# Gates' staging and the top keys' scratch in the solver's spent table

## Chip, core and metric

The kernel runs on one core of a Trainium2 chip. The metric is the device time of one launch in microseconds. TensorE (PE) does the matmuls, VectorE (DVE), ScalarE (ACT) and GpSimd (POOL) the rest; SyncE (SP) and POOL's queue issue transfers.

## The reference, cut to what matters

One decoder block on 512 tokens of width 1024. One projection of the normalised input, `w_in`, gives the columns of three parts: an RWKV-7 token mixer (8 heads of 64), a sparse attention whose keys an indexer chooses, and 2 x 1024 columns of sigmoid gates. Then come cross attention into 256 memory tokens and a mixture of experts.

```python
sa = einsum('bhij,bhj->bhi', state, -kk_t)                  # RWKV: one step per token
state = state * w_t + sa[..., None] * (kk_t * a_t) + v_t[..., None] * k_t
y_t = einsum('bhij,bhj->bhi', state, r_t)                   # then a norm per head, x g
score[t, s] = sum_h w_idx[t, h] * relu(q_idx[t, h] . k_idx[s])   # indexer, 4 heads of 64
keys(t) = the 128 largest scores among s <= t               # min(256, L/4) of L = 512
h = h + (ya @ w_pa * sigmoid(ga + ba) + yb @ w_pb * sigmoid(gb + bb)) @ w_out
```

## The kernel before

**The projections.** `w_in` is used in blocks of 128 columns: 1024 x 128 weights are loaded by SP into a ring of three raw slots in the region "rawring" (`E` in the code), split into a high half by ACT (L197 CAST) and a low half by DVE or, for odd gates, by POOL (L197 TENSOR_TENSOR) into the region "xparts" (`RX`), and multiplied by 24 matmuls of 128x512 (L230).

**The solver.** RWKV runs over 8 chunks of 64 tokens. For each chunk PE does L704 and L710 (right-hand side from the table `AA` and the state), DVE copies it out (L713), PE applies the inverse from the same table `AA` (L716), DVE and ACT each copy half of the answer (L719), and PE forms outputs and the next state (L727, L732), which DVE takes out (L742, L743). `AA` holds for four pairs of heads, all chunks and both heads a 64-column block; L716 of a chunk is the last reader of its blocks. After two chunks each, a group norm runs on DVE and ACT (L753 to L759); PE then transposes y in batches (L768, L157) and multiplies in g2 (L774).

**The indexer.** For query tiles 1, 2 and 3 PE computes scores against 256, 384 and 512 keys (L489), ACT takes the relu (L490), DVE weighs and adds the four heads (L493, L495), POOL masks (L497), and DVE finds the largest keys in 16 rounds of MAX (L501) and MATCH_REPLACE (L502); MAX writes eight values into a scratch tile `m8s`.

**The gates.** Sixteen blocks of columns: projections, tanh on ACT into one of two tiles `gst` (L589), and a transfer to DRAM (`gate_d`, L590) that POOL's queue issues. Between two gates the code lets the indexer go on by three steps (`pace`). Two later parts also use `gst`: the sparse attention's queries (`copy_out`, L777) and keys.

**The memory's norm.** `mem_norm` loads the 256 memory tokens and the vector `norm_mem` (L567) and normalises on DVE (L193).

**Reuse.** Then the regions "rawring" and "xparts" close, and the memory side's regions "early" and "memory" lie over the same bytes. The first load into them is w_uk (L797, on SP), then w_uv and the blocks of w_ck and w_cv; PE transposes the memory (L810) and uses w_uk in L517. A tile of the new regions waits for the last use of every old tile that its bytes overlap, and the regions are tiles as a whole.

**The order.** The instructions of each engine are put in order ahead of time by a scheduler that follows the data dependences and bank use; the program's text gives priorities only. So a changed buffer changes the order on every engine.

Of the kernel before, what the change touches and what calls it, by code (L numbers as in the profile page):

```python
# [8 lines left out]
AF = mybir.ActivationFunctionType  # L9
# [4 lines left out]
T, D, P = 512, 1024, 128  # L14
# [73 lines left out]
def build(tc, I, out):  # L88
    nc = tc.nc
    V, S, G, PE = nc.vector, nc.scalar, nc.gpsimd, nc.tensor  # L90
# [10 lines left out]
    gate_d = park.tile([2, 4, P, 2, T], F32, name="gate_d")  # L101
# [5 lines left out]
    def region(stack, name, n, dt, side=None):  # L107
        return Mem(stack.enter_context(tc.tile_pool(name=name, bufs=1, side=side)).tile([P, n], dt, name=name), n)
# [5 lines left out]
    def psum(tag="mm"):  # L114

        i = turn.get(tag, 0)
        turn[tag] = i + 1
        return PS[:, banks[tag][i % len(banks[tag])], :]
# [117 lines left out]
    E = region(front, "rawring", NX + NK - NR1, F32)  # L236
# [50 lines left out]
    def projT(nb):  # L287
        with tc.issue_after(roots[NT - 1][0]):
            w = ring1.load(I["w_in"][nb], G if nb % 2 else V)
        pt = psum()  # L290
        for k in range(KD):
            mm3(pt[:, :], lambda x: w[:, x, k * P:(k + 1) * P], lambda x: xn[:, k // 4, x, k % 4, :], k == 0, k == KD - 1)
        return pt
# [14 lines left out]
    omm = M.get(14)  # L308
# [8 lines left out]
    hb = M.get(16)  # L317
# [10 lines left out]
    AA = M.get(4, NCH, 2, 64)  # L328
# [121 lines left out]
    bias = {0: cb}  # L450
# [31 lines left out]
    def indexer(qt):  # L482
        nk = (qt + 1) * P
        isc = isc_[qt]
        for h in range(4):
            hr = slice((h % 2) * 64, (h % 2) * 64 + 64)
            rel = rels[h % 2]
            pt = psum("at")
            PE.matmul(pt[:, 0:nk], qiT[hr, h // 2, qt * P:(qt + 1) * P], kiT[hr, 0:nk], start=True, stop=True)  # L489
            S.activation(rel[:, 0:nk], pt[:, 0:nk], AF.Relu)  # L490
            wh = cw[:, qt, P + h:P + h + 1]
            if h == 0:
                V.tensor_scalar(isc[:, :], rel[:, 0:nk], wh, 0.0, op0=OP.mult, op1=OP.add)  # L493
            else:
                V.scalar_tensor_tensor(isc[:, :], rel[:, 0:nk], wh, isc[:, :], op0=OP.mult, op1=OP.add)  # L495
            yield
        G.affine_select(isc[:, qt * P:], isc[:, qt * P:], pattern=[[-1, P]], compare_op=OP.is_ge, fill=NEG, base=0,  # L497
                        channel_multiplier=1)
        m8 = m8s[qt - 1]
        for r in range(16):  # L500
            V.max(m8[:, r, :], isc[:, :])  # L501
            V.match_replace(isc[:, :], m8[:, r, :], isc[:, :], -2.0e38)  # L502
            if r % 2:
                yield
        V.tensor_scalar(isc[:, :], isc[:, :], -2.0e38, BIG, op0=OP.not_equal, op1=OP.mult)
        bias[qt] = isc
        yield
# [56 lines left out]
    def mem_norm():  # L564
        nm, raw = M.get(2, D), E.get(2, D)
        gmem = rels_[:, :]
        nc.sync.dma_start(gmem, I["norm_mem"].partition_broadcast(P))  # L567
        for i in range(2):
            nc.sync.dma_start(raw[:, i, :], I["mem"][i * P:(i + 1) * P, :])
        for i in range(2):  # L570
            norm_tile(nm[:, i, :], raw[:, i, :], gmem)
        raw.done()
        return nm

    def chained(*gens):
        for g in gens:
            yield from g

    def pace(gen, blocks, per):

        for b in blocks:
            b()
            for _ in range(per):
                next(gen, None)

    def gate(nb):
        pt = projT(22 + nb)
        g_ = gst[nb % 2]
        S.activation(g_.ap, pt[:, :], AF.Tanh, scale=0.5, bias=hb[:, nb:nb + 1])  # L589
        nc.gpsimd.dma_start(gate_d[nb // 8, nb % 8 // 2, :, nb % 2, :], g_.ap)  # L590

    def copy_out(nb, dst):
        pt = projT(nb)
        (S.copy if nb % 2 else V.tensor_copy)(dst, pt[:, :])
# [89 lines left out]
    gst = [E.get(T) for _ in range(2)]  # L684
    isc_ = {qt: M.get((qt + 1) * P) for qt in range(1, NT)}
    inverse()
    rels_ = E.get(2 * T)
    rels, m8s = [rels_[:, i * T:i * T + T] for i in range(2)], [E.get(16, 8) for _ in range(3)]
    g2 = M.get(4 * P)
    nc.sync.dma_start(g2[:, :], I["g2"])  # L690

# [6 lines left out]
    for c in range(NCH):  # L698
# [3 lines left out]
        for hp, q in heads:  # L702
            with behind(*first.values()):
                r = PE.matmul(px[own[1 - q], hp * 64:hp * 64 + 64], AA[own[q], hp, c, q, :],  # L704
                              ZV[own[q], c, hp * P + q * 64:hp * P + q * 64 + 64], start=hp == 0, stop=True,
                              skip_group_check=hp > 0)
# [17 lines left out]
        for hp, q in heads:  # L724
            os_ = slice(q * 256 + hp * 64, q * 256 + hp * 64 + 64)
            with behind(*first):
                r = PE.matmul(po[:, os_], ST[:, hp, c, q * 128:q * 128 + 128], ZV[:, c, hp * P + q * 64:hp * P + q * 64 + 64],  # L727
                              start=not first, stop=True, skip_group_check=bool(first))
# [35 lines left out]
    for hp in range(4):  # L764
        pt = psum("rw")
# [14 lines left out]
    latent(projT(17))  # L780
    for i in range(2):
        copy_out(14 + i, qiT[:, i, :])
    bg = chained(*[indexer(qt) for qt in range(1, NT)])
    pace(bg, [lambda i=i: gate(i) for i in range(16)], 3)
    for _ in bg:
        pass
    nm = mem_norm()
    for x in (hb, *gst, rels_, *m8s, omm):
        x.done()
    front.close()  # L790

# [80 lines left out]
    for x, (src, wsrc) in enumerate(((yaT, I["w_pa"]), (ybT, I["w_pb"]))):  # L872
        for k in range(4):
            split(act[:, x, 0, k, :], act[:, x, 1, k, :], src[:, k, :])
        for j in range(4):
# [5 lines left out]
            for n in range(2):  # L881
                nb = j * 2 + n
                pt = psum()
# [604 lines left out]
    with tc.manual_schedule(engines={PE.engine}):  # L1488
# [5 lines left out]
        for p in range(16):  # L1494
# [12 lines left out]
            if p == OVER * 2 + 1:  # L1507
                e = p * 2 + 2
# [80 lines left out]
```

## Time and profile before

| | us |
|---|---|
| median of 3 runs (lowest, highest) | 1271.01 (1266.04, 1273.87) |
| profiled execution: time | 1261.12 |
| profiled execution: span | 1259.3 |
| PE busy, share of the span | 1186.5, 94% |
| DVE busy, share | 647.8, 51% |
| ACT busy, share | 366.6, 29% |
| POOL busy, share | 111.1, 9% |

The span is cut in time by stages: the solver's chunks run from about 230 to 300 us, the gates with the rest of the indexer to 387, the memory side and the sparse attention after it, the experts from about 780 on. In the rows, times count from the span's start; "[1.78 <-DVE xparts L197]" behind an instruction says that its engine stood idle for 1.78 us and what ended that. PEclk is the share of full TensorE clock that was granted. L numbers are lines of the kernel before.

### The profile page before, as it was taken

What the parts mean: (1) busy time and instruction counts of PE and PEld (TensorE: products, weight loads), DVE (VectorE), ACT (ScalarE), POOL (GpSimd) and SP (SyncE); (2) the same over time, 40 slices, a digit from 0 to 9 for tenths busy, and PEclk for the clock granted to TensorE, in tenths of its full rate; (3) what the DMA queues carried; (4) which work ended last, traced back from release to release, by engine and by line L of the source; (5) the groups of instructions that cost most, each with busy time, mean ns of one, the idle gap of its engine ahead of it and who ended that gap; (6) DMA issues with size and microseconds to landing.
All of it is one profiled execution on the core that took longest, in us unless ns stands there. A gap on an engine that the chain in (4) does not pass through costs nothing. (4 is left out here: it accounts for less than half of the span.)

```text
span 1259.3 us, 18869 instructions
## 1 busy us (share of the span) xinstructions
PE 1186.5 (94%) x7630; PEld 860.6 (68%) x7630; DVE 647.8 (51%) x1417; ACT 366.6 (29%) x666; POOL 111.1 (9%) x102
## 2 busy tenths in 40 slices
PE   5999998899998999799999979899999999999995
PEld 5877676677777877688786867566565656565662
DVE  5346689686686563565545373433233333333325
ACT  4442322434333543422444351101010101110113
POOL 1121211111122101200000030000000000000001
PEclk8999898999998999899999989999999999999998
DMA  4211113215533115473324316899999999999991
GB/s 163 91 60 34 54 56 109 79 53 185 193 113 109 55 34 196 155 245 98 131 75 145 128 68 268 337 413 419 419 421 420 420 421 421 419 421 420 362 364 67
DMA packets 52137, 272.06 MB, mean 216 GB/s; under 512 B 6064, under 2 KB 6208, under 8 KB 27728
## 3 DMA queue, kind: packets, MB, share of 16 engines
q1 hardware_dynamic: 48544, 259.21, 53.5%
q0 software_dynamic: 3504, 11.62, 2.6%
q8 instruction: 61, 1.00, 0.3%
q14 instruction: 28, 0.23, 0.1%
HBM read 261.37 MB, written 9.44 MB: 215 GB/s over the span
## 5 line engine op out<-in xcount | busy, mean ns | idle before, releaser
L230 PE MATMUL banks<-xparts 128*128 128x512 f32 x864 | 227.0, 413 | 2.2 <-DVE xparts L197 2.2
L230 PEld LDWEIGHTS banks<-xparts 128*128 128x128 f32 x864 | 164.5, 196 | 43.2 <-issue 3.7
L1452 PE MATMUL banks<-big 128*64 128x256 f32 x1616 | 180.3, 380 | 0.0
L1452 PEld LDWEIGHTS banks<-big 128*64 128x64 f32 x1616 | 115.8, 137 | 63.5 <-issue 8.0
L230 PE MATMUL banks<-weights,rounded 128*128 128x512 f32 x384 | 95.0, 401 | 0.0
L1480 PE MATMUL banks<-big 128*64 128x512 f32 x384 | 86.6, 595 | 1.4 <-issue 1.4
L230 PEld LDWEIGHTS banks<-weights,rounded 128*128 128x128 f32 x384 | 72.0, 191 | 15.2 <-issue 1.0
L1364 DVE TENSOR_TENSOR big<-big,banks 128x512 f32<-128x512 f32 x128 | 79.6, 681 | 4.7 <-PE banks L1362 4.7
L1457 ACT ACTIVATE slot<-banks 128x256 f32<-128x256 f32 x32 | 12.3, 385 | 225.0 <-PE banks L1469 121.1
L197 ACT CAST xparts<-rawring 128x1024 fp32r<-128x1024 f32 x38 | 39.8, 1046 | 121.0 <-PE banks L230 61.3
L1421 PE MATMUL banks<-chosen,rounded 128*128 128x256 f32 x512 | 66.0, 290 | 0.5 <-DVE big L1139 0.3
L197 DVE TENSOR_TENSOR weights<-big,weights 128x1024 fp32r<-128x1024 f32 x32 | 39.0, 1222 | 53.6 <-ACT weights L197 51.2
L1362 PE MATMUL banks<-chosen 128*128 128x512 f32 x256 | 66.5, 403 | 0.0
L1356 DVE SCALAR_TENSOR_TENSOR chosen<-banks,big,chosen 128x512 fp32r<-128x512 f32 x32 | 24.0, 750 | 82.2 <-ACT chosen L1355 82.2
L1421 PEld LDWEIGHTS banks<-chosen,rounded 128*128 128x128 f32 x512 | 64.5, 198 | 2.2 <-DVE big L1438 1.2
L1480 PEld LDWEIGHTS banks<-big 128*64 128x64 f32 x384 | 26.9, 137 | 53.1 <-issue 48.4
L197 POOL TENSOR_TENSOR xparts<-rawring,xparts 128x1024 fp32r<-128x1024 f32 x20 | 48.9, 2446 | 150.4 <-ACT xparts L197 142.7
L1355 ACT ACTIVATE chosen<-banks,big 128x512 fp32r<-128x512 f32 x32 | 22.0, 688 | 131.3 <-PE banks L1480 121.0
L1470 DVE COPY big<-banks 128x512 f32<-128x512 f32 x16 | 11.1, 692 | 89.5 <-PE banks L1469 89.5
L197 ACT CAST weights<-big 128x1024 fp32r<-128x1024 f32 x32 | 33.4, 1051 | 79.6 <-PE banks L230 33.4
L1362 PEld LDWEIGHTS banks<-chosen 128*128 128x128 f32 x256 | 47.7, 192 | 11.9 <-issue 1.6
L1437 DVE TENSOR_SCALAR chosen<-banks,big 128x512 fp32r<-128x512 f32 x16 | 12.0, 751 | 81.9 <-PE banks L1435 81.9
(406 smaller groups left out, 1808.7 us busy)
## 6 DMA issues: line engine op xcount, KB each, us to landing
big<-in_w_e_gate SPq DMA_DIRECT2D x51, 1024.0 KB, 13.5
big<-in_w_e_up SPq DMA_DIRECT2D x50, 1024.0 KB, 13.6
big<-in_w_e_down SPq DMA_DIRECT2D x48, 1024.0 KB, 12.4
rawring<-in_w_in SPq DMA_DIRECT2D x38, 512.0 KB, 3.5
slots<-in_w_e_up SPq DMA_DIRECT2D x14, 1024.0 KB, 15.2
slots<-in_w_e_gate SPq DMA_DIRECT2D x13, 1024.0 KB, 13.4
slots<-in_w_e_down SPq DMA_DIRECT2D x12, 1024.0 KB, 11.7
big<-in_x SPq DMA_DIRECT2D x8, 512.0 KB, 6.4
```

Source lines behind the costliest of these rows:

```text
L197: return S.copy(hi, src).ins, (eng or V).tensor_tensor(lo, src, hi.bitcast(F32), op=OP.subtract).ins
L230: r = PE.matmul(pt, st(a), mv(b), start=(first and i == 0), stop=(last and i == 2))
L1355: r = S.activation(YE[:, 0, nh, :], pd, AF.Copy, scale=g[:, :])
L1356: V.scalar_tensor_tensor(YE[:, 1, nh, :], pd, g[:, :], YE[:, 0, nh, :].bitcast(F32), op0=OP.mult, op1=OP.subtract)
L1362: PE.matmul(pc_[:, :], PT[:, t * P:(t + 1) * P], YE[:, x, nh, :], start=(x == 0), stop=(x == 1))
L1364: V.tensor_add(hh, hh, pc_[:, :])
L1421: PE.matmul(pt[:, 0:256], HL(x, t)[:, k // 4, k % 4, :], Pr_[:, t].rearrange("p e s -> p (e s)"), start=(t == 0 and x == 0), stop=(t == NT ...
L1437: V.tensor_scalar(PT[:, :], pa[:, :], slot_id[:, :], None, op0=OP.is_equal)
L1452: PE.matmul(pu[x][hf * 64:hf * 64 + 64, :], xgs[h4][:, k % 4, es_], w[:, k % 4, hf * 256:hf * 256 + 256], start=(k == 0), stop=(k == KD - 1))
L1457: S.activation(hd_[:, :], pu[0], AF.Silu)
L1470: V.tensor_copy(ht[:], ph[:, :].rearrange("p (j a s) -> p j a s", j=2, s=64))
L1480: PE.matmul(pd[j * 64:j * 64 + 64, :], ht[:, j, fb * 2 + hf, :], w[hf][j][:, fb, nh * 512:nh * 512 + 512], start=(kb == 0), stop=(kb == 3))
```

## The change

The gates' tanh no longer goes to `gst` but to the first pair of heads of the solver's table `AA`: even gates to the half with chunks 0 to 3, odd gates to the half with chunks 4 to 7. The indexer's scratch goes to the second pair of heads. `m8s` is no longer allocated in "rawring"; `gst` stays there for its two other users. The diff:

```diff
@@ indexer
-        m8 = m8s[qt - 1]
+        m8 = spent[1][:, (qt - 1) * P:qt * P].rearrange("p (r e) -> p r e", e=8)
@@ gate
-        g_ = gst[nb % 2]
-        S.activation(g_.ap, pt[:, :], AF.Tanh, scale=0.5, bias=hb[:, nb:nb + 1])
-        nc.gpsimd.dma_start(gate_d[nb // 8, nb % 8 // 2, :, nb % 2, :], g_.ap)
+        g_ = spent[0][:, nb % 2 * T:nb % 2 * T + T]
+        S.activation(g_, pt[:, :], AF.Tanh, scale=0.5, bias=hb[:, nb:nb + 1])
+        nc.gpsimd.dma_start(gate_d[nb // 8, nb % 8 // 2, :, nb % 2, :], g_)
@@ allocation
-    rels, m8s = [rels_[:, i * T:i * T + T] for i in range(2)], [E.get(16, 8) for _ in range(3)]
+    rels = [rels_[:, i * T:i * T + T] for i in range(2)]
@@ before the gates and the indexer
+    spent = [AA[:, i].rearrange("p c x t -> p (c x t)") for i in range(2)]
     bg = chained(*[indexer(qt) for qt in range(1, NT)])
@@ end of the old regions
-    for x in (hb, *gst, rels_, *m8s, omm):
+    for x in (hb, *gst, rels_, omm):
```

Behind the insertion line numbers are two higher in the changed kernel (L797 becomes L799). The change moves instructions on every engine between 190 and 390 us. Below, "xN" counts equal instructions in a row as the program has them.

On PE, in the solver's chunk 3, from L704 to the first projections of the next step. Before:

```order
L704 MATMUL banks<-big 64x64 x8
L230 MATMUL banks<-xparts 128x512
L710 MATMUL banks<-big 64x64
L230 MATMUL banks<-xparts 128x512 x2
L710 MATMUL banks<-big 64x64 x7
L230 MATMUL banks<-xparts 128x512 x4
L716 MATMUL banks<-big 64x64 x8
L230 MATMUL banks<-xparts 128x512 x4
```

Now:

```order
L704 MATMUL banks<-big 64x64 x8
L489 MATMUL banks<-big 128x384
L710 MATMUL banks<-big 64x64 x8
L489 MATMUL banks<-big 128x512
L716 MATMUL banks<-big 64x64 x8
L489 MATMUL banks<-big 128x512
L727 MATMUL banks<-big 128x64
L489 MATMUL banks<-big 128x512 x2
```

The gate projections that stood between the solver's steps are gone from this chunk; in their place stand the scores of query tiles 2 and 3, which came after the solver before.

On DVE, from the copy at the end of chunk 2's L716 to chunk 3's state. Before:

```order
L719 COPY big<-banks 64x4x64
L754 TENSOR_SCALAR big<-big 128x8
L501 MAX rawring<-big 128x8
L755 TENSOR_TENSOR big<-big 128x2x256
L502 MATCH_REPLACE big<-rawring,big 128x256
L501 MAX rawring<-big 128x8
L502 MATCH_REPLACE big<-rawring,big 128x256
L742 TENSOR_TENSOR big<-big,banks 64x256 x2
```

Now:

```order
L719 COPY big<-banks 64x4x64
L495 SCALAR_TENSOR_TENSOR big<-rawring,big 128x256
L493 TENSOR_SCALAR big<-rawring,big 128x384
L501 MAX big<-big 128x8
L495 SCALAR_TENSOR_TENSOR big<-rawring,big 128x384
L502 MATCH_REPLACE big<-big 128x256
L495 SCALAR_TENSOR_TENSOR big<-rawring,big 128x384
L501 MAX big<-big 128x8
L742 TENSOR_TENSOR big<-big,banks 64x256 x2
```

Part of the group norm has gone ahead of the copy, and tile 2's weighing stands among tile 1's search.

On SP's queue, around the first load into the new regions. Before:

```order
L567 DMA rawring<-in_norm_mem 128x1024
L800 DMA big<-q_d 128x512
L223 DMA rawring<-in_w_in 128x1024
L797 DMA early<-in_w_uk 128x512
L798 DMA early<-in_w_uv 128x512
L223 DMA early<-in_w_ck 128x512 x16
```

Now:

```order
L567 DMA rawring<-in_norm_mem 128x1024
L880 DMA big<-in_x 128x1024 x2
L223 DMA rawring<-in_w_in 128x1024
L223 DMA big<-in_w_pa 128x1024
L223 DMA rawring<-in_w_in 128x1024
L880 DMA big<-in_x 128x1024 x2
L223 DMA rawring<-in_w_in 128x1024 x4
L799 DMA early<-in_w_uk 128x512
L800 DMA early<-in_w_uv 128x512
L223 DMA early<-in_w_ck 128x512 x4
L1266 DMA big<-in_w_e_up 128x2048
L223 DMA early<-in_w_ck 128x512 x12
```

norm_mem's load has moved ahead of most of the last loads of w_in, and an expert's load (L1266), which stood much earlier, is now between the loads of w_ck; it writes bytes that `AA` held, so it waits for the last gate's transfer.

## Rows read from the trace of the kernel before

**Rows 1.** Head of the page
```profile
span 1259.3 us, 18869 instructions
```

**Rows 2.** Waits of PE, 190 to 470 us; total, times, longest in us
```profile
PE banks L517 <- DMA early<-in_w_uk: 3.9, 1, 3.9
...
PE banks L230 <- DVE xparts L197: 2.2, 2, 1.8
PE banks L537 <- DVE early L530: 1.6, 2, 0.8
...
PE banks L710 <- DVE big L742: 0.5, 1, 0.5
```

**Rows 3.** Waits of SP's queue, 150 to 560 us
```profile
SPq L797 <- DMA gate_d<-rawring: 26.6, 1, 26.6
```

**Rows 4.** Timeline, start and duration in us; PE alone from 340 to 420
```profile
349.94 11.62 PE L230 MATMUL banks<-xparts 128*128 128x512 f32 x50
363.35 23.48 PE L230 MATMUL banks<-xparts 128*128 128x512 f32 x94 [1.78 <-DVE xparts L197]
...
388.86 0.66 PE L810 MATMUL banks<-big 128*128 128x128 f32 x4 [0.72 <-DVE memory L197]
393.43 3.06 PE L517 MATMUL banks<-big,early 64*128 64x128 f32 x16 [3.91 <-DMA early<-in_w_uk]
```

**Rows 5.** Timeline of all engines, 350 to 405 us
```profile
386.92 0.69 ACT L589 ACTIVATE rawring<-banks,big 128x512 f32<-128x512 f32 x1 [4.75 <-PE banks L230]
...
387.90 0.54 POOL L590 DMA_DIRECT2D gate_d<-rawring  x1 [4.89 <-ACT rawring L589]
...
390.67 0.33 SPq L797 DMA_DIRECT2D early<-in_w_uk  x1
```

**Rows 6.** 1-us windows: length, busy of PE, PEld, DVE, ACT, POOL; PEclk, DMA share, GB/s
```profile
392.00:393.00 1.00, 0.00 (x0) 0.00 (x0) 0.00 (x0) 0.00 (x0) 0.00 (x0) 0.50 0.91 305
...
402.00:403.00 1.00, 1.00 (x9) 0.84 (x8) 0.88 (x4) 0.37 (x2) 0.38 (x1) 0.91 0.01 2
```

**Rows 7.** Windows of 1 us behind the idle before 363.35
```profile
365.00:366.00 1.00, 1.00 (x4) 0.78 (x3) 1.00 (x1) 0.00 (x0) 1.00 (x2) 0.50 0.84 340
...
368.00:369.00 1.00, 1.00 (x6) 0.81 (x5) 0.93 (x4) 0.00 (x0) 0.00 (x0) 0.98 0.00 0
```

**Rows 8.** Timeline of all engines, 358 to 364 us
```profile
360.22 1.28 DVE L193 SCALAR_TENSOR_TENSOR big<-rawring,big 128x1024 f32<-128x1024 f32 x1 [2.02 <-DMA rawring<-in_norm_mem]
```

**Rows 9.** Window of the solver's chunks 2 to 7 and the group norm
```profile
252.00:306.00 54.00, 53.55 (x557) 41.32 (x552) 44.40 (x129) 22.44 (x35) 4.31 (x5) 1.00 0.33 107
```

**Rows 10.** DVE groups, 252 to 306 us: busy, mean ns, idle before and its releaser
```profile
L501 DVE MAX8 rawring<-big 128x8 f32<-128x256 f32 x16 | 6.7, 421 | 0.2
...
L742 DVE TENSOR_TENSOR big<-big,banks 64x256 f32<-64x256 f32 x10 | 4.2, 420 | 2.8 <-PE banks L732 2.6
...
L719 DVE COPY big<-banks 64x256 f32<-64x256 f32 x6 | 2.6, 428 | 1.4 <-PE banks L716 1.3
...
L505 DVE TENSOR_SCALAR big<-big 128x256 f32<-128x256 f32 x1 | 0.2, 242 | 0.0
```

**Rows 11.** DVE's groups of the wide top-key search, 230 to 390 us
```profile
L501 DVE MAX8 rawring<-big 128x8 f32<-128x384 f32 x16 | 8.9, 559 | 0.6 <-POOL big L497 0.3
L502 DVE MATCH_REPLACE8 big<-rawring,big 128x384 f32<-128x384 f32 x16 | 8.7, 542 | 0.0
...
L502 DVE MATCH_VALUE_LOAD big<-rawring,big 128x8 f32 x48 | 4.2, 89 | 1.0
...
L495 DVE SCALAR_TENSOR_TENSOR big<-rawring,big 128x384 f32<-128x384 f32 x3 | 1.8, 611 | 0.0
```

**Rows 12.** Timeline of all engines, 278 to 283 us
```profile
279.24 2.35 POOL L197 TENSOR_TENSOR xparts<-rawring,xparts 128x1024 fp32r<-128x1024 f32 x1 [6.95 <-ACT xparts L197]
279.39 2.23 DVE L186 TENSOR_TENSOR big<-big 128x8 f32<-128x8 f32 x1
```

**Rows 13.** Window of 1 us behind the idle before L537
```profile
409.00:410.00 1.00, 0.76 (x7) 0.55 (x7) 0.54 (x4) 0.00 (x0) 0.09 (x1) 1.00 0.58 199
```

## The prediction

> **What bounds the kernel now.** I read the waits of TensorE (PE) between 190 and 470 us first, then SyncE's (SP) waits, then the timeline where both meet, then one-microsecond windows for the granted clock, and last VectorE's (DVE) load in the stretch where the change reorders work. The profiled execution took 1261.1 us, with a span of 1259.3 [rows 1]; the median of the runs shown is 1271.0, 9.9 above it. The sums below are differences inside that span, and I set them against the median.
>
> Around the change PE is nearly always busy: it has 53.55 of 54 us of work between 252 and 306 [rows 9]. So a microsecond counts only if PE idles for it, or runs slower. PE idles twice where the change can reach [rows 2]: 3.9 us at L517, for w_uk's transfer, and 1.8 us in the gates' projections, for a low half that DVE splits.
>
> The first idle starts on SP. SP waits 26.6 us at L797, and what ends this is the gates' DMA out of the region "rawring" [rows 3]. The last projection ends at 363.35 + 23.48 = 386.83; then come the last tanh on ScalarE (ACT, 386.92), its DMA's issue on GpSimd (POOL, 387.90) and its landing; w_uk's load is issued at 390.67 and L517 starts at 393.43 [rows 4, 5]. From issue to L517 are 2.76 us. PE had been out of work since 388.86 + 0.66 = 389.52.
>
> After this idle PE's granted clock is 0.50, the 1.2 GHz level: it is 0.50 in the window 392 to 393 and 0.91 in 402 to 403 [rows 6]. After the 1.8 us idle that ends at 363.35 it drops too: 0.50 at 365, and 0.98 again at 368 [rows 7].
>
> The second idle's origin is DVE: it waits 2.02 us for the vector norm_mem before L193 [rows 8], and the split that PE needs is queued behind that instruction.
>
> **The junction.** The gates' tiles and the scratch leave "rawring". What is left for w_uk's load to wait for is the last reader of the split weights, the last projection, at 386.83. With 2.76 us to L517 the operand is there at 389.6 against PE's 389.52: about 3.8 of the 3.9 us go. With no long idle the half-clock stretch should go as well: some 8.7 us of PE work from 393.43 on. Were that all bound by PE, full clock would save half, 4.3; were it all latency of ACT and DVE, nothing. The chains there go back and forth between engines, so I take 2.6, a little over half of the upper end. Junction: 6.4 us, from 3.8 to 8.1. In SP's new order an expert's load (L1266) stands behind four of the w_ck loads and waits for the last gate DMA; the twelve w_ck loads behind it need raw slots that come free later anyway, so I cost it at nothing; without that cover it would hold them for the 3.8 us from 386.83 to 390.67 at most.
>
> **The memory's norm.** In SP's new order six loads of w_in come behind norm_mem's, where one did, so it is there long before L193. So the 1.78 us idle goes, and its low clock: 94 projections took 23.48 us where 50 took 11.62 [rows 4], so 94 at the better rate would take 21.8 and the dip cost 1.6. Together 3.4, from 1.8 to 3.8. All gains: 9.8 us.
>
> **The solver's stretch.** Here the change costs. The tanh of gate 0 now writes where the solver's table holds chunks 0 to 3, and waits for chunk 3's L716; gate 1's waits for chunk 7's. The order therefore puts eight L489 groups (scores of the later query tiles) between the solver's steps of chunks 2 and 3 where projections stood, and runs the second tile's top-key search alongside the first's.
>
> PE's work does not grow. From chunk 2's L716 to the second batch of L768, I count 94 projections and the same solver steps: some 53.8 us, against 53.55 [rows 9]. DVE's work grows. In the new order between the same copies (chunk 2's L719 and the last L759) I count ten more MAX and nine more MATCH_REPLACE of 384 wide, and three more L495 (one of them 512 wide, costed as 384). By the durations in [rows 11] this is 10 x 0.559 + 9 x (0.542 + 0.089) + 3 x 0.611 = 13.1 us. DVE's records overlap each other: in the stretch as it is, the busy times of the 24 groups (the first, the last and two between are [rows 10]) add to 49.4 us and the window shows 44.40 busy [rows 9], a factor of 0.90. So 11.8 us are added: 56.2 us of DVE work in 53.8 us of PE work. PE must then wait 2.4 us even if DVE never idles. DVE does idle for PE now: 2.8 us before L742, 1.4 before L719 [rows 10], and 9.6 us in all (54 less 44.40). Were all that idling to stay, PE would lose 56.2 + 9.6 - 53.8 = 12.0. A DVE that is behind rarely waits, so I take 3 us of idling.
>
> POOL takes part too. While POOL's split of an odd gate ran, from 279.24 for 2.35 us, a DVE instruction of eight elements a partition (L186) took 2.23 [rows 12], where copies of 256 take 0.43 [rows 10]. In the stretch there is one such split now and there will be two. I take half a second hold, 1.0. The Trainium skill, "SBUF — State Buffer", section "SBUF: two separate sides", says that DVE with two SBUF operands and GpSimd share one pair of ports as an exclusive lock, held for the whole instruction. Rows 12 agree, and by that rule both splits hold DVE, so the stretch would lose 2.1 and not 1.0.
>
> So PE's new idle is 2.4 + 3 + 1 = 6.4 us, less the 0.5 that it loses at L710 now [rows 2]: 5.9, from 0 (the overlap closer, no idling) to 12.0 + 2.1 - 0.5 = 13.6. The clock I leave alone: an idle of 0.8 us before L537 [rows 2] left it at 1.00 in the window 409 to 410 [rows 13], and my 6.4 us come in six pieces, one for each chunk from the third and one at the norm.
>
> **Sum.** -6.4 - 3.4 + 5.9 = -3.9 us: 1267 against the median of 1271, 1257 against the profiled execution. One per cent, 12.7 us, is about what a measurement of this kernel can tell from no change. The forecast is therefore no measurable change, slightly under before. Nothing behind L517 moves: all engines keep their order there, so what is gained at 393 reaches the end.
>
> **Rivals.**
> - *Slower: DVE becomes the bound in the solver.* The place is L742 and L759, for which PE's L710 and L768 wait. If DVE's idling stays (13.6 us) and four of the waits are long enough to halve the clock, at the 1.6 us that one such dip cost, PE loses 20; less 9.8 this is +10, so 1281; with the low ends of the gains +14, 1285. It decides from 9.8 us of new PE idle upward. For it: 56.2 is above 53.8. Against it: with DVE at 82% in this stretch PE lost only 0.5. The Trainium skill, "TensorE: Matmul & The Clock Gate", section "A second HAM failure mode: psum-queue depth-cycling", says that short idles between groups of matmuls can already make the clock fall back and forth; rows 13 speak against this for a single 0.8 us, and no run here shows a series of them. Chance 0.15 for a time above before, of which 0.05 beyond 1%.
> - *Faster: the fillers hold.* Different top-key searches interleave, DVE keeps up and PE loses nothing: -9.8 - 0.5 = -10.3, so 1261; with the upper ends (8.1 and 3.8) -12.4, 1259. For it: the work on PE is the same, and MAX and MATCH_REPLACE chains that leave gaps alone can fill each other's. Chance 0.13, of which 0.08 measured as over 1%.
> - *The change does not do what it says.* w_uk's load is issued early, but L517 waits for something else as late as the gate DMA was, such as the transfer itself behind other loads. Then the junction gains nothing: -3.4 + 5.9 = +2.5, so 1274. Against it: no transfer is running there (only the gate's), and 2.76 us from issue is a short landing. Chance 0.12.
>
> The forecast case, -9 to 0, has 0.60. The range that should hold the time 8 times in 10 goes from the fast rival's 1259, less 1 for the scatter of the runs, to 1279, between the third rival and the slow one. Faster by over 1%: 0.08; within 1%: 0.86; slower: 0.06.
>
> **What would show it.** Junction: SP's wait at w_uk ends with PE's last projection, the issue stands near 387, L517's idle is under 0.5 us, and the clock stays at 1.00 at 392 to 402 (shifted by what came before). Norm: L193's idle and the 1.8 us before the projections are gone. Stretch: DVE above 95% busy from chunk 2 to the last L759, and new PE waits for DVE of about 6.4 us there, at L716, L710 and L768. The prediction is wrong if these waits are above 12 us or near nothing, if the clock drops there, or if L517 still waits.

## The result

The changed kernel took 1259.69 us (median of 15 runs, 1254.15 to 1282.66) against 1268.36 us of the kernel before (15 runs, 1260.88 to 1274.59): a ratio of 0.9938 with a 95% interval of [0.9916, 0.9960], or -7.9 us of 1268. Less than 1%, as forecast, but about twice the forecast -3.9. Two of the 15 runs, at 1280.4 and 1282.7, are not in that ratio: in the first, which was profiled, TensorE had half clock through most of the solver, the second has nearly the same mean clock (0.943 against 0.944), and with both the mean of the 15 runs is 1262.9 against 1268.3.

The rows of the changed kernel below are of another profiled run of it (1258.7 us, span 1256.9), unless the text says otherwise. L numbers behind 782 are two higher than before. The two spans, 1259.3 [rows 1] and 1256.9, are only 2.4 us apart: the profiled run of the kernel before, at 1261.1, was faster than most of its kind (median 1268.4). So single traces show which waits came and went, and the size of the gain comes from the runs.

PE's waits between 190 and 440 us (total, times, longest in us), to set beside [rows 2]:

```profile
PE banks L727 <- ACT big L719: 1.0, 1, 1.0
PE banks L727 <- DVE big L719: 1.0, 1, 1.0
...
PE banks L823 <- ACT memory L197: 0.9, 1, 0.9
...
PE banks L517 <- DMA early<-in_w_uv: 0.5, 1, 0.5
PE banks L230 <- DVE xparts L197: 0.5, 1, 0.5
PE banks L710 <- DVE big L742: 0.2, 1, 0.2
```

L517 waits 0.5 us where it waited 3.9. L230 waits 0.5 and not 2.2, so the idle of the memory's norm is gone. New are two waits of 1.0 before L727 in the solver, and 0.9 before L823, the first matmul on w_ck.

SP's wait at w_uk, to set beside [rows 3]:

```profile
SPq L799 <- PE banks L230: 14.2, 1, 14.2
```

It is ended by PE's projections. The timeline at the junction (start and duration in us), to set beside [rows 4, 5], first PE alone and then the other engines:

```profile
339.68 50.90 PE L230 MATMUL banks<-xparts 128*128 128x512 f32 x217
...
392.61 0.66 PE L812 MATMUL banks<-big 128*128 128x128 f32 x4 [0.72 <-DVE memory L197]
393.73 1.68 PE L517 MATMUL banks<-big,early 64*128 64x128 f32 x16 [0.47 <-DMA early<-in_w_uv]
```

```profile
390.64 0.33 SPq L799 DMA_DIRECT2D early<-in_w_uk  x1
390.66 0.69 ACT L589 ACTIVATE big<-banks,big 128x512 f32<-128x512 f32 x1 [4.75 <-PE banks L230]
...
391.65 0.54 POOL L590 DMA_DIRECT2D gate_d<-big  x1 [4.90 <-ACT big L589]
```

The last projection ends at 339.68 + 50.90 = 390.58, w_uk's load is issued at 390.64, before the last tanh starts, and L517 follows L812 by 0.47 us. Windows of 1 us behind it (busy by engine, granted clock, DMA share, GB/s):

```profile
394.00:395.00 1.00, 1.00 (x14) 1.00 (x13) 0.61 (x1) 0.11 (x1) 0.00 (x0) 1.00 0.86 311
...
396.00:397.00 1.00, 0.10 (x2) 0.08 (x1) 0.30 (x2) 0.74 (x2) 0.00 (x0) 0.82 1.04 391
397.00:398.00 1.00, 1.00 (x5) 1.00 (x6) 0.00 (x0) 1.00 (x4) 0.99 (x1) 0.50 0.94 293
...
400.00:401.00 1.00, 1.00 (x10) 1.00 (x9) 0.62 (x4) 0.55 (x1) 0.28 (x1) 0.97 0.89 348
```

PE now works at full clock from 393.7 on, but it runs out of work at 396: busy 0.10 with the DMA share at 1.04. It waits for the first block of w_ck, and the clock is at 0.50 for three windows behind that (397 to 400). Before, the half clock lasted from 392 to 402 [rows 6].

The solver's stretch, from chunk 2's L719 to the end of the last L759, to set beside [rows 9] (length, busy of PE, PEld, DVE, ACT, POOL, granted clock, DMA share, GB/s):

```profile
254.80:313.00 58.20, 56.84 (x548) 42.40 (x547) 52.23 (x160) 25.53 (x42) 5.54 (x8) 0.97 0.36 123
```

PE has 1.36 us of idle in 58.2 us, and DVE is busy for 52.23, 90%.

### The profile page after: what moved, and what is told of

It reads as the page before. It is cut to its first block, busy times and chain, and to the rows that moved or that the text cites. A ratio compares the mean times of both kernels' runs of the same rounds, so it can differ in the third digit from the quotient of the medians.

```text
span 1278.6 us, 18863 instructions
## 1 busy us (share of the span) xinstructions
PE 1208.2 (94%) x7630; PEld 874.4 (68%) x7630; DVE 640.3 (50%) x1417; ACT 361.3 (28%) x662; POOL 110.2 (9%) x102
## 5 line engine op out<-in xcount | busy, mean ns | idle before, releaser
L230 PE MATMUL banks<-xparts 128*128 128x512 f32 x864 | 230.5, 419 | 0.6 <-DVE xparts L197 0.5
L230 PEld LDWEIGHTS banks<-xparts 128*128 128x128 f32 x864 | 167.9, 199 | 41.2 <-issue 3.2
L230 PE MATMUL banks<-weights,rounded 128*128 128x512 f32 x384 | 95.1, 401 | 0.0
L230 PEld LDWEIGHTS banks<-weights,rounded 128*128 128x128 f32 x384 | 72.0, 191 | 15.1 <-issue 1.0
L889 PE MATMUL banks<-rounded,weights 128*128 128x512 f32 x192 | 46.3, 405 | 7.5 <-ACT weights L197 7.5
```

Source lines behind the costliest of these rows:

```text
L230: r = PE.matmul(pt, st(a), mv(b), start=(first and i == 0), stop=(last and i == 2))
L889: PE.matmul(pt[:, :], w[:, a, o:o + P], act[:, x, b, k, :], start=(a + b + k == 0), stop=(a == 1 and k == 3))
```

## Experiments

Every ratio is against the kernel before, timed beside it on the same chip; 0.001 is 1.27 us.

**The changed kernel once more**, for its profile.

> The changed kernel once more, for its profile. My theory (junction -6.4, norm -3.4, solver about +2 instead of the +5.9 forecast, since -7.9 was measured): w_uk issued within 0.5 us of the last projection, no half clock behind L517, no 1.8 us idle in the gates, and about 2 to 2.5 us of new PE idle between chunk 1 and the last L759. Rival (the solver costs the forecast 6 us and more is gained behind L517 than forecast): 5 to 7 us of new PE idle there. Rival (the solver costs nothing, junction smaller): under 0.5 us of new idle there.

The new idle is 0.99 before chunk 0's L727, 0.21 before L710 and 1.00 before chunk 5's L727: 2.2 us, the size that my revised theory said, but the first lies a chunk ahead of the stretch that it named, and inside that stretch are 1.2. The forecast's 6.4 us is not there. The theory also misses on "no half clock behind L517": three windows remain.

**Only the last gate back in the old tile.** This undoes the early load and keeps PE's order.

```diff
-        g_ = spent[0][:, nb % 2 * T:nb % 2 * T + T]
+        g_ = gst[1].ap if nb == 15 else spent[0][:, nb % 2 * T:nb % 2 * T + T]
```

> The changed kernel with gate 15 alone staged in the old tile in rawring, so that w_uk's load waits for the last gate's DMA again while PE's order is that of the changed kernel. My theory: it loses the junction alone, +6.4 us against the changed kernel, so about -1.5 us against before (ratio 0.999). Rival (the junction is worth only its idle, 3.8): about -4 us against before (0.997). Rival (the gain comes from the norm and the solver, not from the junction): as fast as the changed kernel, -8 us (0.994).

The order on PE and on DVE is record for record that of the changed kernel. Measured 0.9983 [0.9959, 1.0007], -2.2 us, so the junction is worth 0.9983 - 0.9938 = 0.0045, 5.7 us. The interval excludes the second rival, but it holds both my theory and the first rival (3.8 us). PE's wait for w_uk and the clock are as before the change:

```profile
PE banks L517 <- DMA early<-in_w_uk: 4.0, 1, 4.0
```

```profile
400.00:411.00 11.00, 8.50 (x44) 8.26 (x44) 3.13 (x14) 4.16 (x11) 2.10 (x2) 0.53 0.60 191
```

**Only the last three gates moved**, and the scratch. This gives w_uk its early load, and the order on PE and DVE stays that of the kernel before.

```diff
-        g_ = gst[nb % 2]
+        g_ = gst[nb % 2].ap if nb < 13 else spent[0][:, nb % 2 * T:nb % 2 * T + T]
```

> Gates 13 to 15 and the top keys' scratch in AA, gates 0 to 12 in the old tiles: PE's order through the solver is that of the kernel before, and w_uk's load no longer waits for a gate's DMA. My theory: the junction alone, -6.4 us against before (0.995), with the 1.8 us idle in the gates still there. Rival (junction worth 3.8): -3.8 us (0.997). Rival (the junction gives nothing and the rearrangement gives all): 0 us (1.000).

Measured 0.9978 [0.9951, 1.0006], -2.8 us: short of my -6.4, and the interval holds both rivals, so by itself it settles nothing. Its trace has L517's wait down to 0.4, but the idle of the norm has grown:

```profile
PE banks L230 <- DVE xparts L197: 4.5, 2, 4.0
...
PE banks L517 <- DMA early<-in_w_uk: 0.4, 1, 0.4
```

4.0 us in place of 1.8. PE waits there for a low half that DVE splits, while POOL splits the next block. In the kernel before DVE started first:

```profile
362.08 1.22 DVE L197 TENSOR_TENSOR xparts<-rawring,xparts 128x1024 fp32r<-128x1024 f32 x1
362.11 3.44 POOL L197 TENSOR_TENSOR xparts<-rawring,xparts 128x1024 fp32r<-128x1024 f32 x1 [4.12 <-ACT xparts L197]
```

Here POOL did:

```profile
369.67 2.33 POOL L197 TENSOR_TENSOR xparts<-rawring,xparts 128x1024 fp32r<-128x1024 f32 x1 [4.12 <-ACT xparts L197]
369.83 3.26 DVE L197 TENSOR_TENSOR xparts<-rawring,xparts 128x1024 fp32r<-128x1024 f32 x1
```

Whichever came second took 1 to 2 us longer, and here it was the one that PE needed. The junction's gain is there, and the norm's stall takes part of it back in this trace; how often POOL comes first in the timed runs of either kernel is not known. The next pair has no such stall.

**Only the norm's load early, and the same with the last three gates.** Both kernels have the same order on PE, so their difference is the junction alone, with projections still between the solver's steps. It is close to the order of the kernel before, but not the same: the last score of tile 1 and some projections stand elsewhere. The edit to the kernel before (the second kernel adds the line of the last three gates):

```diff
-        m8 = m8s[qt - 1]
+        m8 = spent[:, (qt - 1) * P:qt * P].rearrange("p (r e) -> p r e", e=8)   # AA[:, 1]
-        gmem = rels_[:, :]
+        gmem = E.get(D).ap
```

> The kernel before with only the scratch in AA and norm_mem in a place of its own in rawring, so that its load is early; the gates stay in the old tiles, so w_uk's load waits for the last gate's DMA. My theory (junction about 5.7 as the pair after / last gate back measured, norm 3.4, solver's rearrangement +1 to 2): -3.4 us against before (0.997), L193's wait gone, L517 still idle for 3.9. Rival (the norm's stall is hidden anyway by what comes after): 0 (1.000).

> The same as the one with the early norm alone, and gates 13 to 15 in AA, so that w_uk's load is early too; TensorE's order is the same in both, and the solver keeps its projections between the steps. My theory: junction and norm without the solver's cost, -5.7 - 3.4 = -9.1 us against before (0.993), 5.7 us below the one with the early norm alone. Rival (junction worth its 3.8 us of idle alone): 3.8 below it. Rival (the rearrangement in the solver is itself a gain, not a cost): slower than the changed kernel by 2 us or more.

Measured 0.9972 [0.9948, 0.9996], -3.5 us, for the norm alone, and 0.9936 [0.9912, 0.9959], -8.1 us, for both; the junction is 0.0036, 4.6 us, between my 5.7 and the rival's 3.8. PE's waits in the first and in the second:

```profile
PE banks L517 <- DMA early<-in_w_uk: 4.0, 1, 4.0
...
PE banks L230 <- DVE xparts L197: 0.5, 1, 0.5
```

```profile
PE banks L823 <- ACT memory L197: 2.2, 1, 2.2
...
PE banks L230 <- DVE xparts L197: 0.5, 1, 0.5
PE banks L517 <- DMA early<-in_w_uv: 0.4, 1, 0.4
```

In the second L823 waits 2.2 us for the split of w_ck's first block: a part of what w_uk's early load brings turns into a wait for the load behind it. This version is as fast as the changed kernel, 0.9936 against 0.9938, with none of its 12 runs above 1264.4.

**Both gate tiles in chunks 0 to 3.**

```diff
-        g_ = spent[0][:, nb % 2 * T:nb % 2 * T + T]
+        g_ = spent[nb % 2][:, 0:T]
```

> Both gate tiles in table blocks of chunks 0 to 3 (two pairs of heads), the scratch in a third pair: the tanh of odd gates no longer waits for chunk 7. My theory: the solver's cost of some 2 us comes from the gap that waiting for chunk 3 opens, which stays: -8 us against before (0.994), within 1.5 us of the changed kernel. Rival (the wait for chunk 7 holds the odd gates and costs): -10 us or better (0.992). Rival (it brings the DVE pile-up back elsewhere): -4 us or worse.

Measured 0.9931 [0.9906, 0.9956], -8.8 us: not to be told from the changed kernel. The wait for chunk 7 costs nothing that these runs can show. Three of its ten runs took 1278 to 1285 us; like the two of the changed kernel they are not in the ratio.

**No tie to the solver at all.** The gates and the scratch go into bytes that were free, and the normalised memory into the table.

```diff
-    spent = [AA[:, i].rearrange("p c x t -> p (c x t)") for i in range(2)]
+    gm8 = M.get(2048)
+    spent = [gm8[:, i * 1024:i * 1024 + 1024] for i in range(2)]
-        nm, raw = M.get(2, D), E.get(2, D)
+        nm, raw = AA[:, 2:4].rearrange("p a c x t -> p a (c x t)"), E.get(2, D)
```

> Both gate tiles and the scratch in free bytes that nothing before used, and the normalised memory in AA in their stead: no tanh waits for the solver at all. My theory: junction and norm, -9 us (0.993), within 2 us of the changed kernel. Rival (tying the gates to the solver's steps costs several us): -11 us or better (0.991). Rival (the normalised memory now waits for the solver's end and makes a new stall): -5 us or worse.

Measured 1.0134 [1.0099, 1.0169], +17 us: worse than every case, and not for the reason of the third, since the memory's norm makes no wait of PE. The rival "DVE becomes the bound", which I had priced for the change itself, happened here. PE's wait, and the window that holds it:

```profile
PE banks L768 <- DVE big L759: 7.5, 1, 7.5
```

```profile
307.00:315.00 8.00, 0.49 (x2) 0.09 (x1) 8.00 (x24) 2.83 (x5) 0.28 (x1) 0.54 0.78 230
```

DVE is busy for all 8 us and PE for 0.49: the searches of all three tiles stand among the group norm, and the transposes that wait for the last L759 follow the solver with almost no projections between. The windows from 307 to 335 have the half clock as well.

**Only the gates moved.**

```diff
-        g_ = gst[nb % 2]
+        g_ = spent[:, nb % 2 * T:nb % 2 * T + T]                                # AA[:, 0]
```

> Only the gates' tiles in AA; the scratch stays in rawring, so w_uk's load also waits for the last MATCH_REPLACE. TensorE's order in the solver is nearly that of the changed kernel and the search ends long before the last projection. My theory: the scratch is no part of it, -8 us (0.994), as the changed kernel. Rival (the scratch holds w_uk's load or the search): -2 to -4 us.

Measured 1.0083 [1.0053, 1.0114], +10.6 us, against both cases, although PE's order in the solver is close to the changed kernel's. The profiled run (1283.4) is the slowest of the eight; the others took 1276 to 1279. Its timeline, and the window that follows:

```profile
252.60 2.35 POOL L197 TENSOR_TENSOR xparts<-rawring,xparts 128x1024 fp32r<-128x1024 f32 x1 [25.09 <-issue]
...
252.86 2.37 DVE L736 TENSOR_TENSOR big<-big 128x256 f32<-128x256 f32 x1
...
255.16 0.47 DVE L495 SCALAR_TENSOR_TENSOR big<-rawring,big 128x256 f32<-128x256 f32 x1
...
255.73 0.49 ACT L490 ACTIVATE rawring<-banks 128x384 f32<-128x384 f32 x1 [0.41 <-DVE big L495]
...
256.23 0.68 PE L716 MATMUL banks<-big 64*64 64x64 f32 x16 [1.44 <-ACT rawring L490]
```

```profile
258.00:286.00 28.00, 28.00 (x163) 18.27 (x164) 13.83 (x41) 7.33 (x13) 0.86 (x2) 0.51 0.13 39
```

POOL's split of a gate's weights starts at 252.60, and DVE's L736, which takes 0.43 elsewhere, takes 2.37. The relu (ACT L490) that needs the product behind it is late, PE idles 1.44 us before L716, and then has a mean clock of 0.51 for 28 us.

**The same, and the changed kernel, with gate 1 split on DVE.**

```diff
-            w = ring1.load(I["w_in"][nb], G if nb % 2 else V)
+            w = ring1.load(I["w_in"][nb], G if nb % 2 and nb != 23 else V)
```

> The kernel with only the gates in AA, which took 10.6 us more than before, with gate 1's low half split on DVE instead of POOL. In its trace POOL's split at 252.6 held a DVE multiplication (L736) for 2.37 us, PE then idled 1.4 us before L716 and stayed at half clock from 258 to 286. If that hold is the cause: no hold, no half clock there, and -6 us or better against before (0.995), like the changed kernel. Rival (the poor filler of chunks 2 and 3, scores in place of projections, makes the half clock by itself): still +5 us or more (1.004).

> The changed kernel with gate 1's low half split on DVE instead of POOL. If POOL's hold is the only danger of the new order: as the changed kernel, -8 us (0.994), with no runs near 1280. Rival (the scores as filler halve the clock without any hold): some runs near 1280 again, or all of them. Rival (the longer DVE queue adds PE waits): -4 us or worse.

Both expectations take the wrong gate. Counted in order, the split at 252.60 is the 26th of the 38, that of gate 3; gate 1's is the 24th, at 225.2. So the edit moves another split, and gate 3's stays on POOL. What it does is to set a new order once more, and in that order L736 starts behind the end of POOL's split; with only the gates moved:

```profile
250.66 2.36 POOL L197 TENSOR_TENSOR xparts<-rawring,xparts 128x1024 fp32r<-128x1024 f32 x1 [35.38 <-ACT xparts L197]
...
253.37 0.43 DVE L736 TENSOR_TENSOR big<-big 128x256 f32<-128x256 f32 x1
```

Measured 1.0009 [0.9984, 1.0035] with only the gates moved, between both cases, and 1.0013 [0.9990, 1.0036] with the whole change, in the last rival's range. In the first the hold and the long half clock are gone and 9.4 us with them. That fits the hold as the cause, but the order changed with it, so it is not shown. The second loses what the change had won, and none of its 12 runs is above 1270.3. PE's waits in it:

```profile
PE banks L727 <- DVE big L719: 2.1, 3, 1.4
PE banks L230 <- ACT big L589: 1.3, 1, 1.3
PE banks L727 <- ACT big L719: 0.5, 1, 0.5
```

These add 3.9 us, and the windows from 282 to 293 have the half clock. PE's order differs from the changed kernel's mainly in chunks 1 to 3, where the scores stand a few steps earlier. The mean granted clock of its runs is 0.958, against 0.964 in the 13 runs of the changed kernel that its ratio rests on; the difference, 0.0057 before rounding, is some 7 us of 1266 (estimate), most of what the second loses. So waits in the solver, and half clock behind them, are real in neighbouring orders.

## Why the prediction was right and where its size was off

| term | forecast | measured |
|---|---|---|
| junction | -6.4 (3.8 to 8.1) | -5.7 (last gate back), -4.6 (pair with the early norm), -2.8 (last three gates, with the norm's longer idle) |
| memory's norm | -3.4 (1.8 to 3.8) | -3.5 (early norm alone, in a slightly different order) |
| solver's stretch | +5.9 (0 to 13.6) | +1.4 (last gate back, less the early norm), +0.2 (the change, less the early norm with the last three gates) |
| sum | -3.9 | -7.9 |

A ratio against the kernel before has an interval of about 3 us to either side, the difference of two such ratios about 4. The sum is no test of the terms: -5.7, -3.5 and +1.4 are differences of the same three ratios and must add up to the measured total.

*The junction* went as told: the wait moved from the gate's DMA to the last projection, the issue to 0.06 us behind its end, and the idle of 3.9 went to 0.5. From the last projection to the end of the span the three traces in which w_uk's load waits for the last gate take 871.3 to 872.7 us, the nine in which it is early 865.9 to 870.7, in the mean 4.0 less. That is nearer to the idle alone (3.8) than to 6.4: the 2.6 us that I took for the clock are not shown at that size. What I left out is what w_uk had hidden: the first block of w_ck, loaded behind it, now ends the next wait (L823, 0.9 here and 2.2 in the kernel with the early norm and the last three gates), and half clock follows in both. It does not follow in every trace: with both gate tiles in chunks 0 to 3 L823 waits 0.6 us and the clock stays up.

*The norm* went as told in mechanism, and the size agrees. The price of its idle is not one number, though: 1.8 us in the trace before and 4.0 in the same order, by whether DVE or POOL started first.

*The solver* is the term that was mis-sized, first in its idle. The step that failed there is "56.2 us of DVE work in 53.8 us of PE work", on both sides. PE first: what needs the last L759 is the second batch of L768, and the cover lasts until PE gets there. I set my count of that work against the window that ends with the last L759 [rows 9], where the kernel before has 2.8 us more before its L768. From the end of chunk 2's L716 to that L768, in the kernel before and in the changed one:

```profile
252.40:308.70 56.30, 55.85 (x555) 42.78 (x554) 44.00 (x128) 23.20 (x36) 4.31 (x5) 1.00 0.36 119
```

```profile
254.60:316.40 61.80, 60.44 (x564) 45.19 (x562) 55.59 (x163) 27.95 (x46) 8.18 (x9) 0.97 0.35 121
```

55.85 us of PE work became 60.44, of which the windows 304 to 308 at half clock hold some 1.7. So the cover was 58.7 us and not 53.8; eight L489 records of 512 (3.4 us busy) are the new part. Then DVE: its groups between chunk 2's L719 and the last L759 add to 61.1 us, near the 49.4 + 13.1 that I had, but they are busy for 52.23, a factor of 0.85 where I took 0.90. The likely reason, which no run tests, is that two searches that do not depend on each other overlap more closely than one search and the norm. DVE was then 90% busy and not above 95%. POOL's split did hold DVE once, the multiplication L495, 1.5 us longer than the 0.48 of its other calls, and it fell at the start of the stretch:

```profile
254.66 2.35 POOL L197 TENSOR_TENSOR xparts<-rawring,xparts 128x1024 fp32r<-128x1024 f32 x1 [28.74 <-ACT xparts L197]
...
255.28 2.01 DVE L495 SCALAR_TENSOR_TENSOR big<-rawring,big 128x256 f32<-128x256 f32 x1
```

DVE's waits for PE stayed as long as in [rows 10]:

```profile
L742 DVE TENSOR_TENSOR big<-big,banks 64x256 f32<-64x256 f32 x10 | 4.2, 419 | 2.5 <-PE banks L732 2.2
...
L719 DVE COPY big<-banks 64x256 f32<-64x256 f32 x6 | 2.6, 428 | 1.3 <-PE banks L716 1.2
```

So 52.2 us of work and 5.8 of waiting fitted into 58.2, and the last L759 ended at 313.0, 3.4 us before L768 at 316.4. (With the last gate back, in the same order, L768 did wait 0.4 us for it.) What PE lost are three short waits, 0.99 before chunk 0's L727, 0.21 and 1.00: 2.2, less the 0.5 of before, 1.7 us. Only the 0.21 stands at a place that I named (L716, L710, L768). Before chunk 5's L727 ACT's copy stood behind the split of a gate's weights. The first of them I had not seen either: on DVE the copy of chunk 0 (L719) now stands behind the first steps of the memory's norm and of tile 1's weighing, which wait for ACT:

```profile
239.88 0.15 DVE L173 TENSOR_SCALAR big<-big 128x1 f32<-128x1 f32 x1 [1.23 <-ACT big L191]
...
240.53 0.43 DVE L719 COPY big<-banks 64x256 f32<-64x256 f32 x1
...
241.02 0.43 PE L727 MATMUL banks<-big 128*128 128x64 f32 x2 [0.99 <-DVE big L719]
```

The second step that failed is "The clock I leave alone". The prediction named a fall of the clock in this stretch as a sign of being wrong, and the clock fell: for 3.4 us from 304.5 in this run, for 51 us in the run at 1280.4. From L661, ahead of chunk 0, to the last projection all twelve traces have the same 1230 matmul records. In the kernel before and in the changed one:

```profile
231.20:386.83 155.63, 153.35 (x1230) 115.66 (x1231) 116.44 (x276) 61.17 (x90) 26.62 (x25) 0.98 0.38 126
```

```profile
232.50:390.58 158.08, 155.73 (x1230) 118.40 (x1231) 112.26 (x276) 56.08 (x86) 25.74 (x25) 0.96 0.35 117
```

| order on PE (traces) | L661 to the last projection, us | of it at half clock, us |
|---|---|---|
| before (before; last three gates) | 155.6; 162.3 | 7; 21 |
| early norm (alone; with the last three gates) | 154.5; 152.0 | 14; 7 |
| the change (1258.7; last gate back; 1280.4) | 158.1; 163.5; 177.2 | 14; 24; 58 |

In the changed kernel's trace this part takes 2.4 us more than before, though the norm's idle is gone, and not by idle, which is 2.3 and 2.4 us, but by half clock. So what the solver cost in the traces is mostly half clock, and that differs between traces of one order. In the runs' mean the cost is small, +1.4 or +0.2 with about 4 to either side; its size stays open.

*The rivals.* "The change does not do what it says" is excluded by the issue at 390.64. "The fillers hold" was the nearer one: -7.9 lies closer to its -10.3 than to my -3.9, so that the range held and the class came out right was in part luck. "DVE becomes the bound" did not come about in the change. Its place was right for one neighbour, L768 behind L759 with 7.5 us without the tie; the +10.6 with the gates alone came by another wait, L716 behind the relu. Its condition was off: I wanted 9.8 us of new idle, and one idle of 1.4 us was followed by 28 us of half clock, one of 0.9 us in the run at 1280.4 by 51.

## What to carry to other kernels

Free the buffer that the next stage's first load waits for, and then look at the second load: it is the next wait. When a buffer change makes a scheduler set a new order, the work moved and the places where fillers go missing decide, and neighbouring orders were 9 us apart here, more by granted clock than by idle; so judge the order and not the edit. Moving only the last few tiles that hold the region, with the one load that was late, gave the same time as moving them all, kept the projections between the solver's steps, and had no run near 1280. And before an experiment is read, look in its trace whether the instruction that it was to move has moved.

## What the runs showed that was not expected

**Half clock while TensorE is busy.** In the run of the changed kernel at 1280.4 us PE idled 0.92 us before chunk 0's L727, and the clock then stayed low for the solver. The same 50 us in that run and in the kernel before:

```profile
244.00:294.00 50.00, 50.00 (x317) 34.29 (x316) 21.63 (x58) 10.83 (x20) 3.50 (x4) 0.51 0.12 33
```

```profile
244.00:294.00 50.00, 49.55 (x583) 39.17 (x578) 39.88 (x116) 20.23 (x32) 6.63 (x6) 1.00 0.17 49
```

PE is never idle in the first, and still at a mean clock of 0.51, with 317 matmuls where the other has 583. In the run of the changed kernel at 1258.7 us nearly the same idle (0.99 us) left the clock at 1.00. With the last gate back, in the same order, idles of 1.22 and 1.00 us at the same two places were each followed by half clock, for 7 us and not for 51. So an idle of this length is followed by a fall in some runs and not in others, and for very different times; what decides stays open. Runs near 1280 came twice in 15 with the change and three times in 10 with both gate tiles in chunks 0 to 3, and not in the 12 with the last gate back or in the 89 of the kernel before (the highest at 1276.4).

**POOL's hold on DVE.** A DVE multiplication of 0.43 us took 2.37 while POOL's split ran. The Trainium skill, "SBUF — State Buffer", section "Who interferes with whom", says that a DVE instruction with two SBUF inputs contends with a GpSimd instruction that reads SBUF; the rows at 252.6 agree, and so do those at 254.66 in the changed kernel, where DVE had the time to spare and PE lost nothing by it. With the last three gates moved, at 369.67, it was the split that PE waited for, and cost 2 us.
